# Short unread products on TensorE at five places of a hybrid decoder layer, and second memory rows transposed later

## The chip, the core and the metric

The kernel runs on one core of one Trainium2 chip. The metric is the device time of one execution in microseconds (us). A core has five engines with an instruction stream each: PE (TensorE: matrix products and transposes; its weight loads are listed as PEld), DVE (VectorE), ACT (ScalarE), POOL (GpSimd) and SP (SyncE, which here issues most transfers). An engine works its stream off in order; semaphores hold an instruction until what it needs from another engine, or from a transfer, has landed.

## What is computed

One decoder layer on 1024 rows of 1024 numbers, in float32. Cut to what matters here:

```
# 1. two head groups that share one input projection (2496 columns) and one output projection
cq, ckv, kpe, rq, rk, rv, rg = split(rms_norm(x) @ w_in)
o_mla = causal_block_attention(q(cq), k(ckv, kpe), v(ckv))      # 4 heads
o_ret = retention_chunkwise(rope(rq), rope(rk), rv) -> norm, gain, * silu(rg)   # 4 heads
x1 = x + concat(o_mla, o_ret) @ w_out
# 2. attention to 256 memory rows
kv = rms_norm(mem) @ w_kv;  q = rms_norm(x1) @ w_q
x2 = x1 + softmax(q k^T) v @ w_o
# 3. router: best of 4 groups, best 2 of its 8 experts; 32 experts of width 256
h = rms_norm(x2)
g_sel = argmax(h @ w_group + b);  top2 of h @ w_expert within the group
out = x2 + sum_e gate_e * ((silu(h @ w_gate[e]) * (h @ w_up[e])) @ w_down[e])
```

## The kernel before

Rows go through in eight blocks of 128. Nearly every product is made of three passes (`mm3`, line 144): a matrix is split into a high part H and a low part L (ACT makes H, DVE makes L), and H*H, H*L and L*H are added up in PSUM. `project` (line 200) does that over eight blocks of 128 inputs for up to 512 columns. Rows are turned by PE with an identity matrix (`transposes`, line 160) into a PSUM bank, from which ACT and DVE write the two parts.

The stages in the order of time, with the times at which the profile shows them:

- Start (`phase_a`, 0 to some 40 us): blocks of x are transposed and multiplied by the 448 columns of the latents. The identity arrives by a transfer.
- Retention (`phase_b`, to about 290 us): four heads of retention. Into the last head the keys of the causal attention are interleaved: `kv_products(tb)` multiplies the latent of block tb (names ckvH, ckvL) by `wk` and leaves raw keys `kn`; `kv_keys` scales and transposes them later. At the end comes `out_part(0, ...)`, line 786: the retention half of the output projection for the first row block, 24 products of 512 columns with weights wh and wl and data oT, under the priority name `bout`.
- Causal attention (`phase_c`, to about 530 us): queries from cq, scores, softmax, values, and the other `out_part`s.
- Memory (`phase_e0` and `phase_e1`, to about 584 us): two blocks of memory rows, normed and transposed into `mT[0]` and `mT[1]`, and their projection in four column chunks; with the first chunk both blocks are multiplied one after the other.
- Cross attention (`phase_e`, from 586.93 us): the first two row blocks of x1 are transposed in two halves (i = 0 and 1), then `queries(0, i)` multiplies them by the query weights, 48 products of 256 columns.
- Router and output (`phase_f`, `choose`, `count`, `route_end`, to about 868 us): for the last pair of row blocks two products with the router's weights `wr`, then DVE picks the experts (`ind`, `oh`), PE counts places with small bf16 products (`trib`, `ones`, into the bank ps_trb), DVE builds A and B, PE multiplies them to the lists of rows (ps_po), and POOL gathers the rows `xg` of the first expert with indirect transfers. Only then can PE transpose xg (`expert_x`, line 1440).
- Experts (`moe`, 868 us to the end): 32 experts, each with transposes of the gathered rows, gate and up products, and the down product.

The order on each engine is not that of the code. A scheduler places the instructions when the kernel is built: it goes by priorities, which the table `PRI` shifts by name (`at`, line 219), by its own estimates of when an operand is there, and by extra order edges (`after`, line 207). A new edge or a new instruction can therefore move many others.

Of the kernel before, what the change touches and what calls it, by code (L numbers as in the profile page):

```python
# [26 lines left out]
BF = mybir.dt.bfloat16  # L27
# [10 lines left out]
NT = 8  # L38
EPS = 1e-6
NE = 32  # L40
# [19 lines left out]
AHEAD = 2  # L60
PRI = {'asq': -60, 'bgate': -20, 'bgate1': -15, 'bnorm': 75, 'bout': 200, 'bproj': 15, 'bproj3': -20, 'btr3': 30, 'ckv': -30, 'cpv': -100, 'cpv3': 5, 'cpv6': 10, 'cq3': 400, 'cq6': -10, 'csm': -5, 'csm6': 10, 'cval': -5, 'e1': -100, 'e1t': -60, 'ebl': 30, 'ecv': -60, 'ecw': 13, 'efn': 15, 'eout': -5, 'eout0': 5, 'eq1': 15, 'eqt': 400, 'esm': -100, 'etr': -5, 'fbeg': -12, 'fbeg1': 100, 'fc0': -20, 'fc02': 10, 'fco': 15, 'fco1': -2, 'fl0': -15, 'fl1': 20, 'fl11': 400, 'fl13': -400, 'ft12': -30, 'ftr': -10, 'ftr1': 2, 'ftr3': 2, 'fwe': -400, 'fwe1': 15, 'fwe2': 20, 'fwe3': 5, 'ma': -200, 'mt': -40, 'outa': -60, 'outa4': 20, 'outa5': 5, 'outr': -105, 'outr5': -5, 'q0': 20, 'wal': 15, 'wap': 100, 'wq': -55}
EO = 2
# [43 lines left out]
class Layer:  # L106
# [37 lines left out]
    def mm3(self, out, sH, sL, mH, mL, start, stop, skip=False):  # L144
        mm = lambda s, m, i, e: self.nc.tensor.matmul(out, s, m, start=i, stop=e, skip_group_check=skip)  # L145
        mm(sH, mH, start, False)
        mm(sH, mL, False, False)
        mm(sL, mH, False, stop)

# [10 lines left out]
    def transposes(self, dst, src, n):  # L160
        for i in range(n):
            self.nc.tensor.transpose(dst[:, i * 128:(i + 1) * 128], src[:, i * 128:(i + 1) * 128], self.ident)

# [67 lines left out]
    def constants(self):  # L231
        nc, a, sm = self.nc, self.a, self.sm
        self.ident = sm.tile([128, 128], F32, name="ident", bufs=1)
        nc.scalar.dma_start(self.ident, a["c_ident"])
        self.mhalf = sm.tile([128, 1], F32, name="mhalf", bufs=1)
        nc.gpsimd.memset(self.mhalf, -0.5)
        warm = sm.tile([128, 1], F32, name="warm", bufs=1)
        nc.gpsimd.tensor_tensor(warm, self.mhalf, self.mhalf, OP.mult)
        nc.gpsimd.tensor_tensor(warm, warm, self.mhalf, OP.pow)
        self.gain = {}  # L240
        self.load_gain("attn_norm_g", 8, nc.scalar)
# [118 lines left out]
    def phase_a(self):  # L360
# [13 lines left out]
        for tb in range(NT):  # L374
# [14 lines left out]
            for i in range(2):  # L389
                cols = slice(i * 512, (i + 1) * 512)  # L390
                tr = self.bank(("tr", "sc")[i])
                self.transposes(tr, xt[i], 4)
                self.split(H[:, cols], L[:, cols], tr)
            self.xT.append([(H[:, k * 128:(k + 1) * 128], L[:, k * 128:(k + 1) * 128]) for k in range(8)])
# [9 lines left out]
        for tb in range(NT):  # L404
            p = self.bank("pj", 448)
            self.project(p, self.xT[tb], wc)
            c = self.slot([128, 512], name=("mr", "xr")[tb % 2], bufs=1, pool=self.O)[:, :448]
            nc.scalar.activation(c, p, AF.Copy, scale=self.r1[:, tb:tb + 1])
            for i, (o, n) in enumerate(((0, 256), (256, 128), (384, 64))):
                self.square(self.css[:, tb, i:i + 1], c[:, o:o + n], p[:, o:o + n])  # L410
            nc.sync.dma_start(self.cd[tb * 128:(tb + 1) * 128, :], c)
            if "c" in self.dbg:
                nc.sync.dma_start(self.dbg["c"][tb * 128:(tb + 1) * 128, :], c)
# [166 lines left out]
    def kv_products(self, tb, role):  # L580
# [9 lines left out]
        p = self.bank(role)  # L590
        self.mm3(p, *cT, *self.wk, True, True)
        p = p.rearrange("p (h c) -> p h c", h=NH)
# [193 lines left out]
    def out_part(self, tb, w, ret, role):  # L786
# [14 lines left out]
        for c in range(2):  # L801
            cols = slice(c * 512, (c + 1) * 512)
            xr = self.slot([128, 512], F32, "xr", 1, self.O) if ret is not None else self.slot([128, 512], F32, "xa", XA)
            nc.sync.dma_start(xr, self.a["x"][0][rows, cols] if ret is not None else self.x1d[rows, cols])
            p = self.bank(role)
            self.project(p, oT, w[c])
            nc.vector.tensor_tensor(xr, p, xr, OP.add)
            nc.sync.dma_start(self.x1d[rows, cols], xr)
            if ret is None:
                self.square(self.sx1[:, tb, c:c + 1], xr, p)  # L810
                if "x1" in self.dbg:
                    nc.sync.dma_start(self.dbg["x1"][rows, cols], xr)
# [9 lines left out]
    def phase_e0(self):  # L822
# [10 lines left out]
        for m in range(2):  # L833
# [7 lines left out]
            self.scaled("mt", mt, mt, sq[:, 3:4])  # L841
            self.mT.append(self.to_T(mt, 8, "mT", 4, pool=self.E0))
        self.ggc = ggc

    def phase_e1(self):
# [45 lines left out]
    def phase_e(self):  # L891
# [20 lines left out]
        def queries(n, i):  # L912
# [142 lines left out]
    def phase_f(self):  # L1055
# [74 lines left out]
        def end(j):  # L1130
# [12 lines left out]
            if last:  # L1143
                column(NT - 1, 1, slice(4, 8), slice(256, 512))
                h = rest()
                for k in range(2):
                    nc.tensor.matmul(pl[:, 1], h[:, k], self.wr[:, 6 + k], start=False, stop=(k == 1),
                                     skip_group_check=True)
                nc.vector.scalar_tensor_tensor(v[:, 1:2], self.s2l, 1.0 / D, v[:, 1:2], OP.mult, OP.add)
# [117 lines left out]
    def choose(self, j):  # L1267
# [26 lines left out]
        V.tensor_tensor(ind, oh[:, :, 0], oh[:, :, 1], OP.add)  # L1294
        pr = self.bank("pr", 2 * NE).rearrange("p (b e) -> p b e", b=2)
        for b in range(2):
            nc.tensor.matmul(pr[:, b], self.ones, self.cum[:, j], start=True, stop=False)
            if b:
                nc.tensor.matmul(pr[:, b], self.ones, ind[:, 0], start=False, stop=False)
            nc.tensor.matmul(pr[:, b], self.trib, ind[:, b], start=False, stop=True)  # L1300
        wr = t([2, NE], "wr2")
# [50 lines left out]
    def list_part(self, pl, j, s, first, last, late=lambda i: i):  # L1352
# [14 lines left out]
        for k in range(4):  # L1367
            nc.tensor.matmul(pl[:CAP, s * NE:(2 * s + 1) * NE], A[:, k // 2, k % 2], B[:, k // 2, k % 2],
                             start=first and k == 0 and s == 0, stop=last and k == 3, skip_group_check=True)

# [15 lines left out]
    def route_end(self):  # L1386
# [3 lines left out]
        pc = self.bank("pr", NE)  # L1390
        nc.tensor.matmul(pc, self.ones, self.cum[:, NT // 2], start=True, stop=True)
        self.cnt = G.tile([128, 1], F32, name="cnt", bufs=1)
# [47 lines left out]
    def expert_x(self, xg):  # L1440
# [3 lines left out]
        for b in range(2):  # L1444
            tr = self.bank("tr")
            for k in range(4):
                nc.tensor.transpose(tr[:, k * CAP:(k + 1) * CAP], xg[:CAP, 4 * b + k::8], self.ident[:CAP, :CAP])
            H, L = [self.M.tile([128, 4 * CAP], F32R, name="x" + s, tag="x" + s, bufs=3) for s in "HL"]
# [253 lines left out]
```

## Time and profile before

| | us |
|---|---|
| median of 3 runs | 1211.96 (1209.45 to 1214.25) |
| the profiled execution, its own time | 1214.96 |
| span in that profile, first to last instruction | 1213.2 |
| TensorE busy in the span | 1162.8 |
| VectorE busy | 771.3 |
| ScalarE busy | 652.3 |
| GpSimd busy | 152.0 |

The profile is of one execution. The span leaves out some 1.8 us around it. The mean granted clock of TensorE over the span is 0.986 of full speed. "Busy" adds up instruction times; PE products overlap one another, so what a product costs is read from the distance of two starts, not from the length of one.

### The profile page before, as it was taken

How to read it: one execution, taken by the hardware profiler on the slowest of the kernel's cores; microseconds unless marked ns; L12 is line 12 of the kernel's file. 1: busy time of each engine (PE TensorE's matmuls, PEld its weight loads, DVE VectorE, ACT ScalarE, POOL GpSimd, SP SyncE). 2: the span in 40 equal slices, each digit the busy share in tenths (PEclk: the TensorE clock that was granted, in tenths of full speed). 3: DMA queues.
4: the chain of work that ended last, by engine and by line, in shares of the span. 5: the costliest groups of instructions: out<-in, count | busy, mean ns of one | idle time of the engine just before them, and what ended most of it. 6: DMA issues, size and time to landing. Idle time of an engine off the chain costs nothing. (4 is left out here: it accounts for less than half of the span.)

```text
span 1213.2 us, 18340 instructions
## 1 busy us (share of the span) xinstructions
PE 1162.8 (96%) x6325; PEld 910.7 (75%) x6325; DVE 771.3 (64%) x1938; ACT 652.3 (54%) x1508; POOL 152.0 (13%) x152
## 2 busy tenths in 40 slices
PE   8999999998999999989999999999699999999995
PEld 7887878776688888878899998778565655566552
DVE  5646464678675786658644445555677777777672
ACT  8723232446554664557644446322477777777672
POOL 1011010121100000000000000000222222222222
PEclk9999999999999999999999999999799999999998
DMA  7622020204323433276611024985799999999982
GB/s 237 181 58 80 11 76 10 89 21 132 100 87 104 153 96 120 81 243 191 218 62 62 27 62 150 314 287 210 263 343 343 342 337 334 315 317 315 320 294 45
DMA packets 115472, 213.23 MB, mean 176 GB/s; under 512 B 20577, under 2 KB 68705, under 8 KB 107185
## 3 DMA queue, kind: packets, MB, share of 16 engines
q1 hardware_dynamic: 106912, 194.59, 47.0%
q0 software_dynamic: 7280, 17.37, 6.2%
q8 instruction: 51, 0.84, 0.3%
q14 instruction: 45, 0.36, 0.1%
q10 hardware_dynamic: 1184, 0.07, 0.1%
HBM read 179.69 MB, written 40.11 MB: 181 GB/s over the span
## 5 line engine op out<-in xcount | busy, mean ns | idle before, releaser
L145 PE MATMUL ps_pj<-wh,xT 128*128 128x512 f32 (+1 forms) x640 | 219.9, 403 | 1.8 <-ACT wh L157 1.2
L158 DVE SCALAR_TENSOR_TENSOR L<-raw,g,H 128x512 fp32r<-128x512 f32 x256 | 180.4, 748 | 55.1 <-ACT H L157 52.2
L157 ACT ACTIVATE H<-raw,g 128x512 fp32r<-128x512 f32 x256 | 169.5, 713 | 32.1 <-PE ps_pj L145 22.7
L145 PEld LDWEIGHTS ps_pj<-wh,xT 128*128 128x128 f32 x640 | 121.1, 190 | 21.1 <-ACT wh L157 1.6
L145 PE MATMUL ps_pj<-wl,xT 128*128 128x512 f32 (+1 forms) x320 | 127.9, 400 | 0.0
L1500 PE MATMUL ps_sc<-raw,aT 128*96 128x512 f32 x256 | 117.6, 602 | 1.2 <-ACT aT L1484 1.0
L145 PE MATMUL ps_pj<-H,xH 128*96 128x512 f32 x256 | 116.2, 454 | 0.0
L145 PE MATMUL ps_pj<-L,xH 128*96 128x512 f32 x256 | 102.6, 401 | 0.1
L145 PE MATMUL ps_pj<-H,xL 128*96 128x512 f32 x256 | 102.0, 398 | 0.0
L1500 PEld LDWEIGHTS ps_sc<-raw,aT 128*96 128x96 f32 x256 | 39.1, 162 | 65.1 <-issue 51.1
L1492 POOL DMA_INDIRECT out_dram<-y,idx x31 | 54.4, 1756 | 201.4 <-ACT H L157 161.6
L145 PE MATMUL ps_pj<-x1TH,wh 128*128 128x256 f32 x256 | 74.3, 290 | 2.6 <-ACT x1TH L154 2.6
L145 PE MATMUL ps_pj<-x1TL,wh 128*128 128x256 f32 x256 | 75.2, 294 | 0.0
L145 PE MATMUL ps_pj<-x1TH,wl 128*128 128x256 f32 x256 | 74.4, 291 | 0.0
L145 PEld LDWEIGHTS ps_pj<-wl,xT 128*128 128x128 f32 x320 | 61.1, 191 | 8.5 <-DVE wl L158 0.5
L145 PEld LDWEIGHTS ps_pj<-H,xH 128*96 128x96 f32 x256 | 42.5, 166 | 22.3 <-issue 7.5
L459 ACT ACTIVATE tg<-ps_pj,rh 128x128 f32<-128x128 f32 x32 | 11.7, 366 | 87.7 <-PE ps_pj L145 87.6
L145 PEld LDWEIGHTS ps_pj<-L,xH 128*96 128x96 f32 x256 | 41.7, 163 | 22.4 <-DVE L L158 8.6
L145 PEld LDWEIGHTS ps_pj<-H,xL 128*96 128x96 f32 x256 | 41.5, 162 | 16.0 <-issue 0.7
L145 PEld LDWEIGHTS ps_pj<-x1TH,wh 128*128 128x128 f32 x256 | 48.4, 189 | 3.0 <-ACT x1TH L154 3.0
L1030 ACT ACTIVATE cP<-ps_sc,cnb,fcq 128x256 f32<-128x256 f32 x32 | 17.8, 561 | 57.9 <-DVE cnb L1025 57.9
L145 PEld LDWEIGHTS ps_pj<-x1TH,wl 128*128 128x128 f32 x256 | 48.6, 190 | 0.0
(412 smaller groups left out, 2882.3 us busy)
## 6 DMA issues: line engine op xcount, KB each, us to landing
raw<-in_expert_w_down_dram SPq DMA_DIRECT2D x32, 1024.0 KB
raw<-in_expert_w_gate_dram SPq DMA_DIRECT2D x32, 1024.0 KB
raw<-in_expert_w_up_dram SPq DMA_DIRECT2D x32, 1024.0 KB
raw<-in_w_in_dram SPq DMA_DIRECT2D x32, 256.0 KB
raw<-in_cross_w_kv_dram SPq DMA_DIRECT2D x32, 256.0 KB
x<-x1d SPq DMA_DIRECT2D x16, 512.0 KB
xr<-in_x_dram SPq DMA_DIRECT2D x16, 256.0 KB
raw<-in_w_out_dram SPq DMA_DIRECT2D x16, 256.0 KB
```

Of the source, the lines that this page charges most:

```text
L145: mm = lambda s, m, i, e: self.nc.tensor.matmul(out, s, m, start=i, stop=e, skip_group_check=skip)
L157: self.high = nc.scalar.activation(H, src, AF.Copy, scale=scale)
L158: return nc.vector.scalar_tensor_tensor(L, src, scale, H.bitcast(F32), OP.mult, OP.subtract)
L459: nc.scalar.activation(tg, p[:, 384:512], AF.Tanh, scale=rh[:, tb:tb + 1])
L1030: nc.scalar.activation(P[:, js], s[:, js], AF.Exp, bias=nb[:, j:j + 1], scale=f[:, j:j + 1], accum_out=su[:, j:j + 1])
L1492: add = lambda c, cs: sums.append(nc.gpsimd.indirect_dma_start(out=out, out_offset=bass.IndirectOffsetOnAxis(ap=rows[:, c:c + 1], axis=0), ...
L1500: nc.tensor.matmul(py[:CAP], act[:, j * CAP:(j + 1) * CAP], wd[:, j, cs], start=(j == 0), stop=(j == 1))
```

## The change

A new helper `idle(out, n, earlier, x)` issues n products of 128x128 whose result nobody reads, into a PSUM bank that is about to be overwritten or lies spare. Its data is the float32 identity, or at the start a bf16 tile `fill` that POOL sets to ones. The first of them is put behind the instruction `earlier` by an order edge. It is called at these places:

1. Start: 24 bf16 products ahead of the first transposes of x, and 8 ahead of the first projection.
2. `out_part` of the first row block of retention: 7 float32 products, ordered behind `self.ckvT`, which is the last product of whichever `kv_products` was emitted last.
3. Memory: 7 behind the transposes of the first memory block, into the bank of the first projection. The transposes of the second memory block move from `phase_e0` into `phase_e1`, behind the emission of the first projection, with the new priority name `mt1`.
4. Cross attention: 8 ahead of the first query products, behind the last transposes.
5. Router: 10 behind the last `wr` products, 3 behind the last place product, 16 behind the product with `cum`; order edges put the work that follows behind them.

```diff
-PRI = {'asq': -60, ...
+PRI = {'mt1': 14, 'asq': -60, ...
...
-            self.nc.tensor.transpose(dst[:, i * 128:(i + 1) * 128], src[:, i * 128:(i + 1) * 128], self.ident)
+            self.lastT = self.nc.tensor.transpose(dst[:, i * 128:(i + 1) * 128], src[:, i * 128:(i + 1) * 128],
+                                                  self.ident)
+
+    def idle(self, out, n, earlier, x=None):
+
+        x = self.ident if x is None else x
+        for _ in range(n):
+            i = self.nc.tensor.matmul(out[:, :128], x, x, start=True, stop=True, skip_group_check=True)
+            if earlier:
+                self.after(i, earlier, "where TensorE waits")
+            earlier = i
+        return i
...
+        self.fill = sm.tile([128, 128], BF, name="fill", bufs=1)
+        nc.gpsimd.memset(self.fill, 1.0)
...
+                if tb == i == 0:
+                    self.idle(tr, 24, None, self.fill)
                 self.transposes(tr, xt[i], 4)
+                if tb == 0:
+                    first = self.lastT
...
+            if tb == 0:
+                self.idle(p, 8, first, self.fill)
             self.project(p, self.xT[tb], wc)
...
-        self.mm3(p, *cT, *self.wk, True, True)
+        self.ckvT = self.mm3(p, *cT, *self.wk, True, True)
...
+            if c == tb == 0 and ret is not None:
+                self.idle(p, 7, self.ckvT)
             self.project(p, oT, w[c])
...
-            self.mT.append(self.to_T(mt, 8, "mT", 4, pool=self.E0))
-        self.ggc = ggc
+            if m == 0:
+                self.mT.append(self.to_T(mt, 8, "mT", 4, pool=self.E0))
+                self.p0 = self.bank("pj")
+                self.idle(self.p0, 7, self.lastT)
+        self.ggc, self.mem1 = ggc, mt
...
-                p = self.bank("pj")
+                p = self.bank("pj") if c or m else self.p0
                 self.project(p, mT[m], wc)
+                if c == m == 0:
+                    with self.at("mt1"):
+                        mT.append(self.to_T(self.mem1, 8, "mT", 4, pool=self.E0))
...
+                if n == 0:
+                    self.idle(p[n], 8, self.lastT)
...
+                self.spare = self.bank("pj")
+                self.idled = self.idle(self.spare, 10, i)
...
+            if last and b:
+                self.after(i, self.idled, "where TensorE waits")
...
+        if last:
+            self.idled = self.idle(self.spare, 3, i)
...
+            if last and s == 0 and self.idled:
+                self.after(i, self.idled, "where TensorE waits")
...
+        i = nc.tensor.matmul(pc, self.ones, self.cum[:, NT // 2], start=True, stop=True)
+        self.idled = self.idle(self.spare, 16, i)
...
+                if self.idled:
+                    self.after(i, self.idled, "where TensorE waits")
+                    self.idled = None
```

Three places show how the order moves on PE. The first is the end of retention. Before, the products with oT of `out_part(0)` begin right behind the key product (ckv) of row block 6, and the chain of the last two blocks (transposes of kn and wk, and what follows) is interleaved with them:

```order
L145 MATMUL ps_pjp<-wh,ckvH 128x512
L145 MATMUL ps_pjp<-wl,ckvH 128x512
L145 MATMUL ps_pjp<-wh,ckvL 128x512
L145 MATMUL ps_pj<-wh,oTH 128x512
L145 MATMUL ps_pj<-wl,oTH 128x512
L145 MATMUL ps_pj<-wh,oTL 128x512
L145 MATMUL ps_pj<-wh,oTH 128x512
L145 MATMUL ps_pj<-wl,oTH 128x512
L145 MATMUL ps_pj<-wh,oTL 128x512
L162 MATMUL ps_trp<-ident,kn 128x128 x4
```

After, PE goes from block 6's key product straight to the chain (transposes of kn, of wk, of the latents, the query products of cq, transposes of qn). Here is the end of that chain, with the key product of block 7 and what stands behind it:

```order
L162 MATMUL ps_trp<-ident,qn 128x128 x2
L145 MATMUL ps_pjp<-wh,ckvH 128x512
L145 MATMUL ps_pjp<-wl,ckvH 128x512
L162 MATMUL ps_trp<-ident,qn 128x128 x2
L145 MATMUL ps_pjp<-wh,ckvL 128x512
L169 MATMUL ps_pj<-ident 128x128 x7
L145 MATMUL ps_pj<-wh,oTH 128x512
L145 MATMUL ps_pj<-wl,oTH 128x512
```

The seven unread products and the 24 products with oT stand behind block 7's key product; the scores of the causal attention that were ahead of it stand behind them.

The second is the entry of cross attention on PE, where x1TH and x1TL are the transposed rows of x1 and x the rows themselves. Before:

```order
L145 MATMUL ps_pj<-wh,mTL 128x512
L145 MATMUL ps_pj<-x1TH,wh 128x256
L162 MATMUL ps_tr<-ident,x_6628 128x128 x4
L162 MATMUL ps_tr<-ident,x_6630 128x128 x4
L145 MATMUL ps_pj<-x1TL,wh 128x256
```

After, in the same place:

```order
L145 MATMUL ps_pj<-wh,mTL 128x512
L162 MATMUL ps_tr<-ident,x_6676 128x128 x4
L162 MATMUL ps_tr<-ident,x_6678 128x128 x4
L169 MATMUL ps_pj<-ident 128x128 x8
L145 MATMUL ps_pj<-x1TH,wh 128x256
L145 MATMUL ps_pj<-x1TL,wh 128x256
```

The first query product no longer stands ahead of the second half's transposes, and the eight unread products lie between these and it.

The third is the router's end on PE (wr: router weights; trib, ones: counting; B and A: lists; xg: gathered rows), after the change; without the rows of line 169 these rows stand as before:

```order
L1176 MATMUL ps_sc<-wr,h 128x36 x2
L169 MATMUL ps_pj<-ident 128x128 x10
L1334 LDWEIGHTS trib
...
L1334 MATMUL ps_trb<-ind,trib 128x32
L169 MATMUL ps_pj<-ident 128x128 x3
L1406 MATMUL ps_po<-B,A 96x32 x4
L1431 LDWEIGHTS ones
L1431 MATMUL ps_trb<-cum,ones 128x32
L169 MATMUL ps_pj<-ident 128x128 x16
L1488 MATMUL ps_tr<-ident,xg_10031 128x96 x8
```

Each group stands ahead of the instruction that waited before.

## Rows read from the trace of the kernel before

**Rows 1.** Page, busy us of each engine, share of the span, instructions:

```profile
PE 1162.8 (96%) x6325; PEld 910.7 (75%) x6325; DVE 771.3 (64%) x1938; ACT 652.3 (54%) x1508; POOL 152.0 (13%) x152
```

**Rows 2.** TensorE's waits: total us, times, longest; six of the longest:

```profile
PE ps_tr L1447 <- DMA xg<-x2d,src: 4.1, 1, 4.1
PE ps_tr L162 <- DMA ident<-in_c_ident_dram: 3.9, 1, 3.9
PE ps_trb L1300 <- DVE ind L1294: 3.1, 1, 3.1
PE ps_pj L145 <- DVE oTL L155: 2.7, 1, 2.7
PE ps_pj L145 <- ACT x1TH L154: 2.6, 1, 2.6
PE ps_pj L145 <- ACT mTH L154: 2.4, 1, 2.4
...
PE ps_po L1368 <- DVE A L1359: 1.3, 1, 1.3
```

**Rows 3.** Windows: start:end, length, busy us by engine, then PEclk, DMA:

```profile
283.30:304.90 21.60, 17.65 (x91) 14.24 (x92) 17.32 (x54) 10.41 (x35) 3.48 (x4) 0.92 0.53 173
304.90:320.00 15.10, 12.43 (x67) 8.38 (x65) 10.64 (x36) 9.00 (x31) 1.08 (x2) 1.00 0.26 94
...
340.00:520.00 180.00, 176.99 (x1134) 154.57 (x1133) 123.12 (x324) 96.30 (x246) 5.04 (x5) 1.00 0.34 109
...
584.30:590.00 5.70, 3.11 (x15) 2.95 (x15) 4.01 (x7) 4.08 (x8) 0.00 (x0) 0.70 0.50 162
...
861.00:868.30 7.30, 1.29 (x9) 0.97 (x8) 6.16 (x31) 2.68 (x5) 3.50 (x3) 0.50 0.62 209
868.30:873.60 5.30, 5.26 (x24) 4.05 (x24) 3.81 (x10) 2.13 (x4) 2.96 (x4) 0.54 0.90 243
```

**Rows 4.** Timeline of the start, TensorE: start us, length, operation:

```profile
11.50 0.57 PE L145 MATMUL ps_pj<-wh,xT 128*128 128x448 f32 x1
11.87 1.05 PE L162 MATMUL ps_sc<-ident,xin 128*128 128x128 f32 x4
```

**Rows 5.** The same stretch on ScalarE, idle time in brackets:

```profile
11.36 0.60 ACT L154 ACTIVATE xT<-ps_tr 128x512 fp32r<-128x512 f32 x1 [0.91 <-PE ps_tr L162]
...
12.96 0.60 ACT L154 ACTIVATE xT<-ps_sc 128x512 fp32r<-128x512 f32 x1 [1.00 <-PE ps_sc L162]
```

**Rows 6.** Timeline of TensorE, end of retention:

```profile
290.22 0.40 PE L145 MATMUL ps_pj<-wh,oTH 128*128 128x512 f32 x1
290.45 0.40 PE L145 MATMUL ps_pj<-wl,oTH 128*128 128x512 f32 x1
...
294.12 0.38 PE L481 MATMUL ps_sc<-w 128*128 128x128 f32 x2
294.34 0.39 PE L489 MATMUL ps_st<-w,wk 128*128 128x128 f32 x2
...
295.59 0.38 PE L162 MATMUL ps_tr<-ident,wk 128*128 128x128 f32 x2
...
304.54 0.48 PE L145 MATMUL ps_pjp<-wh,ckvL 128*128 128x512 f32 x1
```

**Rows 7.** Timeline of TensorE, first memory products:

```profile
536.16 0.78 PE L145 MATMUL ps_pj<-wh,mTH 128*128 128x512 f32 x1
...
538.80 0.39 PE L145 MATMUL ps_pj<-wh,mTH 128*128 128x512 f32 x1
```

**Rows 8.** Timeline of TensorE, entry of cross attention:

```profile
587.34 1.97 PE L162 MATMUL ps_tr<-ident,x 128*128 128x128 f32 x8
...
590.06 0.28 PE L145 MATMUL ps_pj<-x1TH,wh 128*128 128x256 f32 x1
```

**Rows 9.** Timeline of TensorE, counting products of the router:

```profile
861.02 0.19 PE L1297 MATMUL ps_trb<-cum,ones 128*128 128x32 bf16 x1
861.05 0.19 PE L1299 MATMUL ps_trb<-ind,ones 128*128 128x32 bf16 x1
```

More of the change, by code (lines that the diff above doesn't have):

```diff
@@ L60 @@
 AHEAD = 2
-PRI = {'asq': -60, 'bgate': -20, 'bgate1': -15, 'bnorm': 75, 'bout': 200, 'bproj': 15, 'bproj3': -20, 'btr3': 30, 'ckv': -30, 'cpv': -100, 'cpv3': 5, 'cpv6': 10, 'cq3': 400, 'cq6': -10, 'csm': -5, 'csm6': 10, 'cval': -5, 'e1': -100, 'e1t': -60, 'ebl': 30, 'ecv': -60, 'ecw': 13, 'efn': 15, 'eout': -5, 'eout0': 5, 'eq1': 15, 'eqt': 400, 'esm': -100, 'etr': -5, 'fbeg': -12, 'fbeg1': 100, 'fc0': -20, 'fc02': 10, 'fco': 15, 'fco1': -2, 'fl0': -15, 'fl1': 20, 'fl11': 400, 'fl13': -400, 'ft12': -30, 'ftr': -10, 'ftr1': 2, 'ftr3': 2, 'fwe': -400, 'fwe1': 15, 'fwe2': 20, 'fwe3': 5, 'ma': -200, 'mt': -40, 'outa': -60, 'outa4': 20, 'outa5': 5, 'outr': -105, 'outr5': -5, 'q0': 20, 'wal': 15, 'wap': 100, 'wq': -55}
+PRI = {'mt1': 14, 'asq': -60, 'bgate': -20, 'bgate1': -15, 'bnorm': 75, 'bout': 200, 'bproj': 15, 'bproj3': -20, 'btr3': 30, 'ckv': -30, 'cpv': -100, 'cpv3': 5, 'cpv6': 10, 'cq3': 400, 'cq6': -10, 'csm': -5, 'csm6': 10, 'cval': -5, 'e1': -100, 'e1t': -60, 'ebl': 30, 'ecv': -60, 'ecw': 13, 'efn': 15, 'eout': -5, 'eout0': 5, 'eq1': 15, 'eqt': 400, 'esm': -100, 'etr': -5, 'fbeg': -12, 'fbeg1': 100, 'fc0': -20, 'fc02': 10, 'fco': 15, 'fco1': -2, 'fl0': -15, 'fl1': 20, 'fl11': 400, 'fl13': -400, 'ft12': -30, 'ftr': -10, 'ftr1': 2, 'ftr3': 2, 'fwe': -400, 'fwe1': 15, 'fwe2': 20, 'fwe3': 5, 'ma': -200, 'mt': -40, 'outa': -60, 'outa4': 20, 'outa5': 5, 'outr': -105, 'outr5': -5, 'q0': 20, 'wal': 15, 'wap': 100, 'wq': -55}
 EO = 2
@@ L147, in mm3 @@
         mm(sH, mL, False, False)
-        mm(sL, mH, False, stop)
+        return mm(sL, mH, False, stop)
     def split(self, H, L, src, scale=None):
@@ L1146, in end @@
                 for k in range(2):
-                    nc.tensor.matmul(pl[:, 1], h[:, k], self.wr[:, 6 + k], start=False, stop=(k == 1),
-                                     skip_group_check=True)
+                    i = nc.tensor.matmul(pl[:, 1], h[:, k], self.wr[:, 6 + k], start=False, stop=(k == 1),
+                                         skip_group_check=True)
+                self.spare = self.bank("pj")
+                self.idled = self.idle(self.spare, 10, i)
                 nc.vector.scalar_tensor_tensor(v[:, 1:2], self.s2l, 1.0 / D, v[:, 1:2], OP.mult, OP.add)
@@ L1295, in choose @@
         pr = self.bank("pr", 2 * NE).rearrange("p (b e) -> p b e", b=2)
+        last = j == NT // 2 - 1
         for b in range(2):
-            nc.tensor.matmul(pr[:, b], self.ones, self.cum[:, j], start=True, stop=False)
+            i = nc.tensor.matmul(pr[:, b], self.ones, self.cum[:, j], start=True, stop=False)
+            if last and b:
+                self.after(i, self.idled, "where TensorE waits")
             if b:
                 nc.tensor.matmul(pr[:, b], self.ones, ind[:, 0], start=False, stop=False)
-            nc.tensor.matmul(pr[:, b], self.trib, ind[:, b], start=False, stop=True)
+            i = nc.tensor.matmul(pr[:, b], self.trib, ind[:, b], start=False, stop=True)
+            if last and not b:
+                self.after(i, self.idled, "where TensorE waits")
+        if last:
+            self.idled = self.idle(self.spare, 3, i)
         wr = t([2, NE], "wr2")
@@ L1367, in list_part @@
         for k in range(4):
-            nc.tensor.matmul(pl[:CAP, s * NE:(2 * s + 1) * NE], A[:, k // 2, k % 2], B[:, k // 2, k % 2],
-                             start=first and k == 0 and s == 0, stop=last and k == 3, skip_group_check=True)
+            i = nc.tensor.matmul(pl[:CAP, s * NE:(2 * s + 1) * NE], A[:, k // 2, k % 2], B[:, k // 2, k % 2],
+                                 start=first and k == 0 and s == 0, stop=last and k == 3, skip_group_check=True)
+            if last and s == 0 and self.idled:
+                self.after(i, self.idled, "where TensorE waits")
     def list_rows(self, pl):
@@ L1390, in route_end @@
         pc = self.bank("pr", NE)
-        nc.tensor.matmul(pc, self.ones, self.cum[:, NT // 2], start=True, stop=True)
+        i = nc.tensor.matmul(pc, self.ones, self.cum[:, NT // 2], start=True, stop=True)
+        self.idled = self.idle(self.spare, 16, i)
         self.cnt = G.tile([128, 1], F32, name="cnt", bufs=1)
@@ L1446, in expert_x @@
             for k in range(4):
-                nc.tensor.transpose(tr[:, k * CAP:(k + 1) * CAP], xg[:CAP, 4 * b + k::8], self.ident[:CAP, :CAP])
+                i = nc.tensor.transpose(tr[:, k * CAP:(k + 1) * CAP], xg[:CAP, 4 * b + k::8], self.ident[:CAP, :CAP])
+                if self.idled:
+                    self.after(i, self.idled, "where TensorE waits")
+                    self.idled = None
             H, L = [self.M.tile([128, 4 * CAP], F32R, name="x" + s, tag="x" + s, bufs=3) for s in "HL"]
```

## The prediction

> **What bounds the kernel now.** I read the page first: TensorE is busy for 1162.8 of 1213.2 us [rows 1], so only some 50 us of its time are idle, and work added to its stream counts unless it lies in such an idle time. The list of its waits says where these are [rows 2]. Six of them are the five places of the change: 4.1 us for the gathered rows xg, 3.9 for the identity, 3.1 for ind, 2.7 for oTL, 2.6 for x1TH, 2.4 for mTH; 1.3 for A lies between the two of the router. Then windows around these places show the granted clock [rows 3]. It is 0.50 in 861 to 868.3 and 0.54 in 868.3 to 873.6, where TensorE is busy for 5.26 of 5.3 us; 0.70 in 584.3 to 590; 0.92 over 283.3 to 304.9; 1.00 in the long causal stage, whose 180 us hold 177 of work. So behind a wait TensorE works at half its pace for a few us, and a wait costs more than its length. That is what a fill could win; a fill can't end the waits, which end on transfers, DVE or ACT. Last I read timelines there for prices, and the order of the instructions, since the scheduler has placed them anew.
>
> **Prices.** At full pace a product of 512 columns takes 0.23 us from start to start (290.22 to 290.45) [rows 6], at half pace 0.44 (six in 2.64 us from 536.16 to 538.80) [rows 7]. A float32 128x128 product, two passes, takes 0.22 at full pace (294.12 to 294.34) [rows 6], so I put 0.44 at half pace. No row has a bf16 product of 128 columns. Those of 32 columns start 0.03 apart at a granted clock of 0.50 [rows 9, 3]; four times the columns gives 0.12 as an estimate. The upper bound is a float32 transpose of 128 columns at about half pace, 0.25 (eight in 1.97) [rows 8].
>
> **1, the start.** The 24 products need only a small POOL fill, and by 0.12 each they take 2.9 us, inside the 3.9 us wait for the identity; by 0.25 they take 6.0 and end some 2.5 us late, which is the bound of loss. Another 8 lie behind the transposes, where PE would wait for ACT to split them. What can be won: at 11.50 a product of 448 columns takes 0.37, half pace against 512 columns in 0.23 [rows 4, 6]. ACT there waits twice for PE's transposes, 0.91 and 1.00 us [rows 5]; with PE at full pace these go. Later ACT is what is late, so no more than the two is won. I take **-1.9** (range -2.6 to +2.5).
>
> **2, the end of retention.** Here the order decides. The fills are tied to the last `kv_products` emitted, which is block 7's, not block 6's after which the 2.7 us wait stood. So the wait is not filled: the seven fills and the 24 products with oT behind them now stand at the end of the chain of the last two blocks. Before, these 24 were what TensorE did while that chain went through DVE, ACT and POOL: 24 x 0.231 = 5.5 us from 286 on. The chain can't speed up by as much: its transposes of wk ran at 295.59, and these wait for DVE's rotations, whose order there is the same as before. Block 7's key product ends the chain; its last pass started at 304.54 [rows 6]. Without the twelve score passes and the others that the new order puts behind it, 1.6 us earlier: about 302.9. Then 7 x 0.22 = 1.55 and 5.5: 310 us. By 304.9 the kernel before had also done some 2.5 us of scores and other products that now stand behind. The lag is 310 - 304.9 + 2.5 = 7.6 us at full pace; with idle time left in the chain the clock may fall, and at half pace the fills and the first products bring it to 12. What can be caught up afterwards: 304.9 to 320 has 15.10 - 12.43 = 2.67 us of idle time, and 340 to 520 has 3.0 [rows 3]; I take 1 off. 6.6 and 11, weighted two to one: **+8** (range +5 to +12).
>
> **3, the memory.** Seven fills (1.5 us at full pace, 3.1 at half) go into the 2.4 us wait for mTH [rows 2], which ends on ACT's split of the transposes. The products after it lost 2.64 - 6 x 0.23 = 1.25 us by the pace [rows 7]. The second block's eight transposes are issued anyway; between products they cost no more than before. The gain may be lost at the wait for x1TH, if a transfer sets that: 0 to -1.7, I take **-1.2**.
>
> **4, entry of cross attention.** In the new order all eight transposes of the second half come first, then the eight fills, then the products. The fills are not in the 2.6 us wait [rows 2] but behind it. At half pace 8 x 0.44 = 3.5 us; the pace in the trace returned at 590.06, the seventh product [rows 8], so a part runs at full: transposes to 588.9, fills to about 591.2. By then the kernel before had done 16 products, some at half pace, that now take 16 x 0.12 = 1.9. I take **+2**. At full pace (1.8 us of fills, less about 1.1 of faster transposes) it is +0.7.
>
> **5, the router.** At full pace 10 fills take 2.2, 3 take 0.66, 16 take 3.5 us; the waits are 3.1, 1.3 and 4.1 [rows 2], so they are covered. At half pace the sixteen need 7.0 and the transposes of xg come 2.9 us late; the ten need 4.4 and add 1.3 more. The gain is the half pace after 868.3: 5.26 x (1 - 0.54) = 2.4 us [rows 3]. If the pace doubles within the sixteen, they end about 0.9 late, and -2.4 + 0.9 = **-1.5** (range -2.4 to +4.2).
>
> On the profile's clock the Trainium skill has a rule, TensorE: Matmul & The Clock Gate, section Terms: the penalty of throttling is about the throttled time times what the clock lacks of full. By that rule, an estimate, 584.3 to 590 would give back 5.7 x 0.30 = 1.7 us, 861 to 873.6 some 7.3 x 0.50 + 5.3 x 0.46 = 6.1; the trace does not bear out the second, because TensorE was busy for only 1.29 us of the first 7.3 [rows 3], and the pace lost while waiting costs nothing. By the rule in place of my terms for these two places the sum would be 5.4 - 3.7 - 4.6 = -2.9, or 1209.1 in the median, no change that can be told; it falls together with the rival of a neutral order and shares its chance.
>
> **Sum.** -1.9 + 8 - 1.2 + 2 - 1.5 = +5.4, against the profiled execution of 1214.96: 1220.4. That execution is 3.0 above the median of 1211.96, so I forecast 1220.4 - 3.0 = **1217.4**, about 0.45% slower. A measurement of this kernel can tell about 0.5%, 6.06 us: below 1205.9 is faster, above 1218.0 slower.
>
> **Rivals.**
> - *The fills do what they say and the new order costs nothing.* The end of retention gives -1.6 (the pace lost from 286 to about 290), the entry of cross attention -1.5 by overlap with its wait, the others their best: -2.6 - 1.6 - 1.7 - 1.5 - 2.4 = -9.8, so 1205.2 and **1202.2** in the median. For it: half pace stands behind each wait [rows 3]. Against it: the order at two places. It decides for faster as long as place 2 costs less than about +2.1.
> - *The new order is neutral*: the 24 products fill later idle time as well as they filled the chain. Place 2 is 0, the rest as in the sum: -2.6, **1209.4**. For it: the causal stage has other idle spots, and DVE (17.32 of 21.60 us) is nearly the bound at the end of retention [rows 3].
> - *The fills don't raise the pace.* Short products leave the clock where it was; they run at half pace: 0 + 11 + 0 + 2.2 + 4.2 = +17.4, so **1229.4** in the median. For it: at 868.3 TensorE worked nearly without a gap for 5 us at a mean of 0.54 [rows 3]. It decides at place 5, if the sixteen aren't over when xg lands.
>
> **Chances.** My forecast 0.48, with its own range 1213 to 1222: 0.21 of it slower by over 0.5%, 0.27 within. Half pace 0.10, all slower. Neutral order 0.21: 0.17 within, 0.04 faster. Fills as meant 0.21, faster. Together: faster 0.25, same 0.44, slower 0.31. The range 1203 to 1226 leaves out most of the half-pace case and about half of the best one, 0.18.
>
> **What the profile after would show.** Place 2: TensorE's idle time between block 6's and block 7's key products grows from 4 us (21.60 - 17.65 [rows 3]) to about 10, and the products with oT start near 304 instead of 286. Place 4: the wait for x1T stays at about 2.5, now before a transpose or the fills, and the first product starts near 591. Place 1: ACT's two waits gone, the 448-column products 0.20 apart before 12. Place 5: the clock of the 5 us after xg lands near 1, the wait for xg filled. The prediction is wrong if the products with oT, though late, leave the causal stage's end where it was, or if the sixteen delay xg's transposes by more than the pace gives back.

## The result, and the profile after

The changed kernel takes 1229.59 us (median of 6 runs, 1227.16 to 1233.32) against 1212.51 of the kernel before (6 runs): a ratio of 1.0142, with a 95% interval of 1.0123 to 1.0161. That is 17 us slower, above the end of the range (1226). The profiled execution after has a span of 1227.5 us (1229.36 with what lies around it), 14.3 more than before.

Where the time comes in is read from the first use of a few tiles: the scores of the causal attention (qTH), the memory products (mTH), the query products of cross attention (x1TH), the gathered rows (xg). Here are these rows of the kernel before, by tile (min, median and longest time of one in ns, then the starts of the first and the last in us):

```profile
L145 PE MATMUL ps_sc<-kv,qTH x160: 274/283/388, 302.2 to 503.8; 128*128 128x256 f32 x160
L145 PE MATMUL ps_pj<-wh,mTH x64: 392/394/776, 533.8 to 583.5; 128*128 128x512 f32 x64
L145 PE MATMUL ps_pj<-x1TH,wh x256: 277/282/583, 586.9 to 736.6; 128*128 128x256 f32 x128
L1447 PE MATMUL ps_tr<-ident,xg x256: 246/274/427, 868.3 to 1179.2; 96*128 96x96 f32 x128
```

And of the changed kernel:

```profile
L145 PE MATMUL ps_sc<-kv,qTH x160: 274/282/562, 318.9 to 520.7; 128*128 128x256 f32 x160
L145 PE MATMUL ps_pj<-wh,mTH x64: 392/394/494, 550.6 to 598.8; 128*128 128x512 f32 x64
L145 PE MATMUL ps_pj<-x1TH,wh x256: 278/282/369, 604.5 to 752.8; 128*128 128x256 f32 x128
L1488 PE MATMUL ps_tr<-ident,xg x256: 246/274/349, 883.2 to 1193.9; 96*128 96x96 f32 x128
```

The first scores come 16.7 us later, and the first memory product 16.8 later. Behind that the distance goes up and down and shrinks in the end: 15.3 at the last memory product, 17.6 at the first query product, 16.2 at the last one, 14.9 at the gathered rows. The last pass of block 6's key product, at the end of retention, still comes 0.4 us earlier than before (282.45 against 282.89). So the loss arises between that product and the memory products, which is where place 2 stands, and the other places together look like a gain of some 2 us in these two executions. The stretch between the two points, before and then after (columns as in [rows 3]):

```profile
282.89:533.75 250.86, 237.33 (x1454) 201.27 (x1452) 171.92 (x477) 135.16 (x371) 12.73 (x14) 0.99 0.37 121
282.45:550.62 268.17, 247.18 (x1483) 210.69 (x1481) 172.42 (x477) 136.45 (x371) 12.94 (x14) 0.95 0.35 113
```

It is 17.3 us longer. Of these, 7.5 us are idle time of TensorE and 9.8 are busy time: the unread products that lie in it, and products that ran at the lower clock.

The six long waits [rows 2] are gone from the top of the list of waits; others stand there now (us in total, times, longest):

```profile
PE ps_trp L162 <- DVE kn L627: 5.4, 2, 3.9
PE ps_fl L145 <- DVE xr L828: 3.0, 3, 1.9
PE ps_trp L162 <- DVE kv L155: 3.0, 2, 1.7
PE ps_trp L162 <- ACT qn L667: 2.6, 2, 1.3
PE ps_trp L162 <- DVE kv L158: 2.2, 3, 1.6
PE ps_tr L162 <- DVE x1TL L155: 1.9, 1, 1.9
...
PE ps_tr L1488 <- DMA xg<-x2d,src: 0.4, 1, 0.4
```

The waits for kn, kv and qn are those of the chain at the end of retention and of its continuation. Before, the 24 products stood in this time, and what was left to wait was shorter (0.79 us for qn at 299.54). The wait for xg shrank from 4.1 us to 0.4, because unread products lie in it, and the rows still come no earlier.

TensorE's timeline at place 2, after:

```profile
282.45 0.39 PE L145 MATMUL ps_pjp<-wh,ckvL 128*128 128x512 f32 x1
286.75 0.98 PE L162 MATMUL ps_trp<-ident,kn 128*128 128x128 f32 x4 [3.91 <-DVE kn L627]
...
294.80 0.69 PE L162 MATMUL ps_tr<-ident,wk 128*128 128x128 f32 x2 [0.85 <-DVE wk L493]
...
305.70 0.69 PE L162 MATMUL ps_trp<-ident,qn 128*128 128x128 f32 x2 [1.30 <-ACT qn L667]
...
307.65 0.78 PE L145 MATMUL ps_pjp<-wh,ckvL 128*128 128x512 f32 x1
308.23 2.97 PE L169 MATMUL ps_pj<-ident 128*128 128x128 f32 x14
310.95 0.48 PE L145 MATMUL ps_pj<-wh,oTH 128*128 128x512 f32 x1
...
316.50 0.60 PE L162 MATMUL ps_trp<-ident,kn 128*128 128x128 f32 x4
318.66 0.44 PE L162 MATMUL ps_trp<-ident,krt 128*128 128x128 f32 x2 [1.56 <-DVE kv L158]
318.85 0.48 PE L145 MATMUL ps_sc<-kv,qTH 128*128 128x256 f32 x2
```

The first row is the end of block 6's key product. Behind it TensorE waits 3.9 us for kn, does the chain with gaps and at half pace, and reaches the unread products (14 passes for 7) at 308.23, the products with oT at 310.95 and the end of them at 316.50. Windows of this stretch and of the router's end (columns as in [rows 3]):

```profile
282.80:311.00 28.20, 18.39 (x66) 13.70 (x65) 16.78 (x56) 12.68 (x43) 3.38 (x4) 0.58 0.25 80
311.00:325.00 14.00, 10.71 (x56) 9.07 (x56) 5.41 (x11) 2.68 (x6) 1.01 (x1) 0.88 0.26 94
...
883.20:888.50 5.30, 5.16 (x34) 4.16 (x35) 4.56 (x14) 2.69 (x5) 3.47 (x4) 1.00 0.86 243
```

Against [rows 3], idle time at the end of retention grew from 4.0 to 9.8 us and the granted clock fell from 0.92 to 0.58; behind it another 3.3 us are idle. At the router the clock of the 5.3 us after xg lands is 1.00 in place of 0.54: there the unread products do what they should.

What the other engines do meanwhile shows in ScalarE's first step after the chain, and VectorE's:

```profile
317.13 0.69 ACT L157 ACTIVATE kv<-ps_trp,ggn 128x512 fp32r<-128x512 f32 x1 [6.55 <-PE ps_trp L162]
```

```profile
317.86 0.75 DVE L158 SCALAR_TENSOR_TENSOR kv<-ps_trp,ggn,kv 128x512 fp32r<-128x512 f32 x1 [3.19 <-ACT kv L157]
```

While TensorE works through the unread products and the 24 products, ScalarE stands for 6.55 us for a transpose of kn that is queued behind them, 8.85 us behind the key product's last pass (316.50 against 307.65). Before, the 24 products were done by 294.12, and these transposes came 2.0 us behind that pass (306.50 against 304.54), so ScalarE's wait was short:

```profile
307.17 0.69 ACT L157 ACTIVATE kv<-ps_trp,ggn 128x512 fp32r<-128x512 f32 x1 [0.56 <-PE ps_trp L162]
```

### The profile page after: what moved, and what is told of

Read it like the earlier page. It is cut to its first block, busy times and chain, and to the rows that moved or that the text cites. A ratio compares the mean times of both kernels' runs of the same rounds, so it can differ in the third digit from the quotient of the medians.

```text
span 1227.5 us, 18608 instructions
## 1 busy us (share of the span) xinstructions
PE 1178.0 (96%) x6459; PEld 925.2 (75%) x6459; DVE 771.4 (63%) x1938; ACT 653.8 (53%) x1508; POOL 154.6 (13%) x153
## 5 line engine op out<-in xcount | busy, mean ns | idle before, releaser
L145 PEld LDWEIGHTS ps_pj<-x1TL,wh 128*128 128x128 f32 x256 | 48.3, 189 | 0.0
```

## The experiments

**The place at the end of retention alone, or left out.** Three kernels. `no2` is the changed kernel without it:

```diff
-            if c == tb == 0 and ret is not None:
-                self.idle(p, 7, self.ckvT)
```

> The changed kernel without the seven products at the end of retention (place 2); the other four places stay. Theory, the order at place 2: what was lost came from tying these products, and with them the 24 products with oT, behind block 7's key product. Then this kernel has the trace's differences of the other places alone: about -0.4 at the start, -1.4 at the memory, +0.8 at the entry of cross attention, -0.9 at the router, so -2 of the kernel before, 1210 to 1211, ratio 0.997 to 0.999. Rival, the loss is spread (unread products anywhere cost, or moving the memory transposes does): it stays above 1218, ratio over 1.005.

`only2` is the kernel before with these lines, `ckvT` and `idle`, and nothing else of the change.

> The kernel before with place 2 alone: seven unread products tied behind block 7's key product. Theory, the order at place 2: the whole loss and the small gains of the other places given back, 1229 to 1232, ratio 1.014 to 1.016. Rival, the loss is spread over the places: under 1222, ratio under 1.008.

`one` is `only2` with one unread product in place of seven:

```diff
-                self.idle(p, 7, self.ckvT)
+                self.idle(p, 1, self.ckvT)
```

> As the kernel with place 2 alone, but with one unread product in place of seven; on TensorE the order is else the same. Theory, the order: the place is what costs, six products fewer give back 2.3 us at the 0.39 that they took, so 1226 to 1229. Rival, the unread products themselves cost (their time, or their PSUM bank): most of the loss goes, under 1218.

Measured: `no2` 1.0008 (0.9995 to 1.0020), `only2` 1.0130 (1.0104 to 1.0156), `one` 1.0116 (1.0096 to 1.0135). The whole loss is this place, and it is the tie and not the products: with one product it is nearly the same. In the traces the products take 1.99 us in `only2` (308.07 to 310.06) and 0.28 in `one` (308.06 to 308.34), so six more are 1.7 us; the ratios are 0.0014 apart, which is as much, but their intervals overlap. The range expected of `only2`, 1.014 to 1.016, was missed by a little, and the one of `no2`, 0.997 to 0.999, too: the other four places gave no gain together, so the 2 us that the two traces above seemed to show lie within what two executions differ by.

**The tie moved along the chain.** Where the products with oT are tied was changed. `block6` ties the seven behind block 6's key product, just ahead of the wait:

```diff
-        self.ckvT = self.mm3(p, *cT, *self.wk, True, True)
+        i = self.mm3(p, *cT, *self.wk, True, True)
+        if tb == 6:
+            self.ckvT = i
```

> As the kernel with place 2 alone, but the seven products are tied behind block 6's key product, which stands just ahead of the 2.7 us wait for oTL; the 24 products with oT stay where they were in the kernel before. Theory, the order: the loss is gone, and the half pace from 286 to 290 with it if the products raise the clock: 1209 to 1213, ratio 0.997 to 1.001. Rival, any extra edge or product here makes the scheduler lay out the causal attention anew, and that is what costs: over 1220, ratio over 1.006.

`mid0` and `mid` have one unread product tied inside the chain, behind the transposes of cq (`cqT`) and behind its first six products (in the same line, `cq0`):

```diff
-                self.idle(p, 7, self.ckvT)
+                self.idle(p, 1, self.cqT)
```

> Place 2 alone with one unread product, tied not behind block 7's key product but earlier in the same chain, behind the transposes of the latents cq (at 295 us in the kernel before). The 24 products with oT follow it. Theory, the cover: these products were the work that TensorE did while the chain of the last two blocks went through the other engines; tied here they leave the first 10 us of the chain bare and still cover its second half, so the loss is about half of that with the tie behind block 7: 6 to 9 us, ratio 1.005 to 1.008. Rival, any tie that takes the products out of their place makes the scheduler lay out what follows worse, however far it takes them: 1.010 to 1.013 as with the tie behind block 7.

> As mid0, but tied behind the first six query products of cq (some 299 us with the chain at half pace). Theory, the cover: more of the chain is bare than in mid0 and less than with the tie behind block 7: 8 to 12 us, ratio 1.007 to 1.010, and above mid0. Rival: 1.010 to 1.013, equal to mid0.

Measured, with the start of the first product with oT from each trace:

| tied behind | products with oT from | ratio (95%) |
|---|---|---|
| nothing (before) | 286.02 us | 1 |
| block 6's key product, 7 products | 289.92 | 1.0033 (1.0017 to 1.0050) |
| transposes of cq, 1 product | 297.17 | 1.0076 (1.0052 to 1.0101) |
| six products of cq, 1 product | 299.42 | 1.0083 (1.0061 to 1.0105) |
| block 7's key product, 1 product | 308.34 | 1.0116 (1.0096 to 1.0135) |
| block 7's key product, 7 products | 310.06 | 1.0130 (1.0104 to 1.0156) |

The loss grows with the distance, from 4 us for 3.9 to 14 for 22.3. Neighbours in the table can't be told apart, since their intervals overlap; but all eight times of `mid0` and `mid` (1219.0 to 1225.6) lie below all eight of `one` and `only2` (1225.8 to 1233.2), against medians of the kernel before that are 0.3 us apart. That is what the cover theory says; the rival, that any tie which takes the products out of their place costs the same, falls. A weaker rival stays. In each of these kernels TensorE also does the causal attention in another order than before, with the same products. The cost doesn't follow how far that reaches: the old order is back from 379 us on in `mid0`, and only from 473 on in `block6`, which lost less. But what the new order costs by itself was not isolated.

The tie that was expected to cost nothing, `block6`, also cost 4 us (2.1 to 6.1), between the ranges of its theory and its rival. A part of the reason is in its trace:

```profile
283.16 0.39 PE L145 MATMUL ps_pjp<-wh,ckvL 128*128 128x512 f32 x1
286.29 2.73 PE L169 MATMUL ps_pj<-ident 128*128 128x128 f32 x12 [2.74 <-DVE oTL L155]
288.82 1.06 PE L162 MATMUL ps_trp<-ident,kn 128*128 128x128 f32 x4
289.67 0.49 PE L169 MATMUL ps_pj<-ident 128*128 128x128 f32 x2
289.92 0.47 PE L145 MATMUL ps_pj<-wh,oTH 128*128 128x512 f32 x1
```

The unread products don't lie in the wait: they start when it ends, at 286.29, with the same 2.74 us before them that the real products had [rows 2]. They write a bank of ps_pj, of which the kernel has three in this stage (`self.psum(pj=3, ...)`). VectorE's steps that read ps_pj there:

```profile
285.46 0.68 DVE L155 TENSOR_TENSOR oTL<-ps_pj,oTH 128x512 fp32r<-128x512 f32 x1
287.73 0.28 DVE L484 TENSOR_TENSOR wk<-ps_pj,sn 128x128 f32<-128x128 f32 x1
288.00 0.28 DVE L474 SCALAR_TENSOR_TENSOR sg<-tg,ps_pj 128x128 f32<-128x128 f32 x1
```

TensorE wrote nothing else to ps_pj between 282.9 and 286.29, so the last two still read older products, and two banks were held beyond 286.29. The one that came free is that of the first row: the unread products waited for the step that makes oTL, as the real ones did. So they fill nothing and push the first product with oT back by 3.6 us. That push is not the whole account of the 4 us: block 7's key product comes only 1.5 us later than before (305.47 against 303.93), and further on another stretch of this trace is at half pace,

```profile
317.00:324.00 7.00, 6.50 (x22) 5.11 (x23) 3.99 (x10) 2.98 (x9) 0.00 (x0) 0.51 0.39 121
```

where the clock before was 1.00. (Such a stretch can be chance: the same window is at 0.76 in the trace of `only4`, below, whose order on TensorE is that of before up to there.) How the loss divides between the two is open. Whether another bank would have let the products into the wait was not tried.

**The half pace in the bare chain.** `warm20` is `one` with the second column half of the products tied as well, and 20 more unread products that the scheduler may lay between the chain's instructions:

```diff
-            if c == tb == 0 and ret is not None:
-                self.idle(p, 1, self.ckvT)
+            if tb == 0 and ret is not None:
+                if c == 0:
+                    self.idle(p, 20, self.ckv6)
+                self.idle(p, 1, self.ckvT)
```

> As the kernel with one unread product behind block 7's key product, the second column half of the 24 products tied there too, and 20 more unread products laid by the scheduler into the first half of the bare chain (from 286 to about 292 us), where TensorE went at half pace. Theory, the pace: the half pace in the chain is a good part of the loss beside the missing cover; with the first half at full pace block 7's key product starts 1.5 to 3 us before 306, and the ratio falls to 1.007 to 1.010. Rival, the chain waits for the other engines and the pace matters little: block 7's key product stays at 306 to 308, ratio 1.011 to 1.014 as with one product.

Measured 1.0079 (1.0054 to 1.0103). The windows of the same stretch, of `warm20`:

```profile
282.80:308.00 25.20, 17.46 (x99) 14.06 (x98) 16.99 (x55) 11.96 (x40) 3.38 (x4) 0.90 0.28 94
```

and of `one`:

```profile
282.80:308.00 25.20, 14.91 (x51) 10.46 (x51) 15.93 (x54) 10.19 (x34) 3.38 (x4) 0.61 0.29 90
```

The clock rose from 0.61 to 0.90, and block 7's key product came only 1.3 us earlier (first pass, of `warm20` and then of `one`):

```profile
304.91 0.47 PE L145 MATMUL ps_pjp<-wh,ckvH 128*128 128x512 f32 x1 [0.24 <-DVE rt L540]
```

```profile
306.22 0.76 PE L145 MATMUL ps_pjp<-wh,ckvH 128*128 128x512 f32 x1
```

The ratio is in the theory's range, but the key product is a little later than the theory had it. Part of what the pace gave was taken on the way there, since the transposes of cq, in the middle of the chain, came later in `warm20`. They are shown for `one` and then for `warm20`:

```profile
295.44 0.63 PE L162 MATMUL ps_trp<-ident,cq 128*128 128x128 f32 x2
```

```profile
296.16 0.44 PE L162 MATMUL ps_trp<-ident,cq 128*128 128x128 f32 x2 [0.16 <-DVE ckvL L155]
```

From there to the key product the chain took 10.8 us in `one` and 8.8 in `warm20`, against 8.1 in the kernel before (295.81 to 303.93), so in that half the pace is some 2 us. The ratio fell by 0.0037, or 4.5 us, but the two intervals overlap. The stretch from block 6's key product to the first memory product, of `one` and then of `warm20`:

```profile
282.63:548.12 265.49, 242.90 (x1457) 206.61 (x1455) 172.43 (x477) 136.16 (x371) 12.93 (x14) 0.95 0.36 114
```

```profile
282.90:546.49 263.59, 243.16 (x1499) 208.34 (x1497) 172.59 (x477) 136.13 (x371) 12.92 (x14) 0.99 0.36 115
```

Against the kernel before, `one` is 14.6 us longer there, 9.1 of idle and 5.6 of busy time; `warm20` is 12.7 longer, 6.9 and 5.8: its clock is nearly that of before, but its 21 further unread products are busy time too. So idle time is the larger part of the loss. How much of the 14 us is pace was not settled: the traces show 1.3 to 2 us of it, and the ratios leave room for 4.5.

**The other places, one at a time.** Each is the kernel before with one place of the change, cut from its diff: `only1` the start, `only3` the memory, `only4` the entry of cross attention, `only5` the router. The first added line of each, in this order:

```diff
+                    self.idle(tr, 24, None, self.fill)
...
+                self.idle(self.p0, 7, self.lastT)
...
+                    self.idle(p[n], 8, self.lastT)
...
+                self.idled = self.idle(self.spare, 10, i)
```

> The kernel before with place 1 alone: 24 and 8 unread bf16 products at the start. The four places other than the end of retention gave 1.0008 together, so each is small or they cancel. My term for this one was -1.9 us (ratio 0.998); the trace of the changed kernel shows the end of retention only 0.4 us earlier, which would be 0.9996. Theory, what is won ahead of a stage that ScalarE or a transfer bounds is given back: 0.999 to 1.001. Rival, my term: 0.997 to 0.999.

> The kernel before with place 3 alone: seven unread products in the wait for the first memory block, and the second block's transposes moved behind the first projection. My term was -1.2 us (ratio 0.999). Theory, the products after it do run at full pace, but the first of them starts later, because more of its stream now stands ahead: 0.999 to 1.001. Rival, my term in full or more: 0.997 to 0.999.

> The kernel before with place 4 alone: eight unread products behind the second half's transposes, ahead of the first query products. My term was +2 us (ratio 1.0017), since they stand behind the wait. Theory, the eight transposes already bring the pace back, and the eight products only add themselves: 1.000 to 1.002. Rival, they give back the half pace of the first query products in full: 0.998 to 0.999.

> The kernel before with place 5 alone: 10, 3 and 16 unread products in the router's waits. My term was -1.5 us (ratio 0.9988), from half pace after the gathered rows land. Theory, the profile shows that gain at the first expert's products, but the experts that follow are bound by more than TensorE's start: 0.999 to 1.001. Rival, my term in full: 0.997 to 0.999.

Measured: `only1` 0.9998 (0.9986 to 1.0009), `only3` 0.9999 (0.9990 to 1.0007), `only4` 1.0018 (1.0005 to 1.0030), `only5` 0.9992 (0.9980 to 1.0004). Two show no difference, one a loss of 2.2 us, and 1.0 us at the router may be nothing. In the trace of `only1` the gain at the start is there, and is given back on the way:

```profile
L145 PE MATMUL ps_sc<-kv,qTH x160: 277/283/387, 299.8 to 503.2; 128*128 128x256 f32 x160
L145 PE MATMUL ps_pj<-wh,mTH x64: 392/394/794, 534.1 to 584.4; 128*128 128x512 f32 x64
```

The first scores come 2.4 us earlier than before, the last 0.6 earlier, and the first memory product 0.3 later, behind a wait for mTH that is now 3.3 us long. By this trace, what is won ahead of the causal attention is taken by waits in it and behind it; but that is likely and not shown, since the last scores come at 506.2 in the execution of `only5` and at 503.8 in that of the kernel before, with the same order up to there. `only4`, where before the seventh product started at 590.06 [rows 8]:

```profile
588.59 1.78 PE L162 MATMUL ps_tr<-ident,x 128*128 128x128 f32 x8 [4.00 <-DVE x1TL L155]
590.16 3.16 PE L169 MATMUL ps_pj<-ident 128*128 128x128 f32 x16
593.08 0.36 PE L145 MATMUL ps_pj<-x1TH,wh 128*128 128x256 f32 x1
```

The unread products stand behind the wait and take 2.9 us of their own. The wait ahead of them is 4.0 us long in this trace, against 2.6 before.

**The fourth place moved into its wait.** `four_early` is `only4` tied behind the last memory product:

```diff
-                    self.idle(p[n], 8, self.lastT)
+                    self.idle(p[n], 8, self.kvlast)
```

> Place 4 alone, with its eight unread products tied behind the last product of the memory projection in place of the last transposes, so that seven of them stand inside the wait for x1TH and not behind it. Theory, the position: the +2 us of place 4 are the products behind the wait; here the wait covers them: 0.999 to 1.001. Rival, the new order of transposes and first products at this place costs by itself: 1.001 to 1.003 as before.

Measured 1.0003 (0.9988 to 1.0018): no loss is left that can be told, though the interval still reaches the 1.0018 of `only4`, and no gain took its place. Its trace has them where they should be:

```profile
585.66 1.72 PE L169 MATMUL ps_pj<-ident 128*128 128x128 f32 x14
587.22 0.60 PE L162 MATMUL ps_tr<-ident,x 128*128 128x128 f32 x4
```

**Versions without what loses.** `p135` has the start, the memory and the router; `p1345e` also the fourth place as in `four_early`.

> The kernel before with the places that did not lose by themselves: the start, the memory, the router. If their measured ratios multiply: 0.9998 x 0.9999 x 0.9992 = 0.9989, between 0.997 and 1.000. Rival, what one wins another wait takes: 0.9995 to 1.001.

> The start, the memory and the router as changed, and the entry of cross attention with its products tied behind the last memory product, inside the wait; the end of retention as before. If the measured ratios multiply: 0.9988 x 1.0003 = 0.999, between 0.997 and 1.0005, clearer than without place 4 only if the pace at that entry counts. Rival, the place is worth nothing or less there: over 1.0.

Measured 0.9988 (0.9975 to 1.0001) and 0.9988 (0.9974 to 1.0003). Both are at the product of the single ratios; both intervals reach 1, so a gain of 1.5 us is likely and not shown.

## Why the prediction was wrong

The direction was forecast and the place was the right one: the tie to block 7's key product leaves the chain of the last two blocks bare. The step that failed is the size of **term 2**, +8 with a range of +5 to +12; alone it measures 1.0130, or +15.8 us (12.6 to 18.9). By its own steps:

- "About 302.9" for the last pass of block 7's key product, from which the fills were counted. That pass starts at 307.65 and the fills at 308.23, 5.3 us later. I took the times of the kernel before and subtracted the work that the new order puts behind, as if the chain got shorter by it. But TensorE waits in it for other engines: twice 1.30 us for qn and 0.85 for wk. From the transposes of cq to the first pass of the key product the chain took 8.1 us before; in `warm20`, near full pace, it took 8.8, so the 1.6 us that I subtracted did not come off. In the changed kernel it took 11.1 (295.28 to 306.38), and the 2.3 us on top of 8.8 are the half pace, which I had put on the fills and the first products and not on the chain.
- "7 x 0.22 = 1.55 and 5.5". The seven took 2.72, at half pace for the most part; the 24 took 5.55 (310.95 to 316.50), as worked out. So these end at 316.5 and not at 310. Put into the prediction's own formula that is 316.5 - 304.9 + 2.5 = 14.1 us, in place of 7.6 at full pace and 12 at half.
- "I take 1 off" for what is caught up afterwards. Nothing shows that it was: the place alone measures 15.8. ScalarE stood still for 6.55 us while the 24 products ran, and when they were over, TensorE waited again for kv: 3.3 us idle from 311 to 325. I had looked for idle time on TensorE that the late work could use, and not for work of ScalarE and VectorE that is queued behind it. That this makes up the rest of the miss is likely and not shown.
- The two cases, full pace 6.6 and half pace 11, were both too low; the weighting between them was not what failed. The rival with half pace gave 1229.4, near the measured 1229.6, but that is luck: it put +11 on place 2, +4.2 on the router and +2.2 on place 4, and at the router the clock did rise.

The other terms against what each measures alone: the start -1.9, measured -0.2 (-1.7 to +1.1); the memory -1.2, measured -0.1 (-1.2 to +0.8); the entry of cross attention +2, measured +2.2 (0.6 to 3.6); the router -1.5, measured -1.0 (-2.4 to +0.5). The sum of the single measurements is +16.7, and the change measures +17.1, so the places add up. **Term 4** was right in size and reason, as the position behind the wait shows. **Term 3** is neither borne out nor refuted: in the trace of `only3` the memory products take 48.9 us from the first to the last, in place of 49.7, and -1.2 lies at the edge of the interval. **Term 5** was right about the clock (0.54 to 1.00), and its -1.5 lies in the interval; from the first transposes of xg to the first down product it is 16.1 us before, 14.9 in `only5` and 14.6 in the changed kernel. By the Trainium skill's rule for the penalty (TensorE: Matmul & The Clock Gate, section Terms), worked out ahead as an estimate of 6.1 us for that stretch, the gain would have been several times what was measured (1.0, at most 2.4); the prediction's reading of the trace, that pace lost while waiting is worth nothing, agrees with it. **Term 1** failed as a sum over a stage's own waits: in `only1` ScalarE's two waits shrank from 0.91 and 1.00 us to 0.16 and 0.25, and block 6's key product came 1.3 us earlier, but the kernel's time did not show it; by that trace it came back as a longer wait 230 us later.

What the profile was to show: the idle time of place 2, said to be about 10 us, is 9.8; the products with oT, said to start near 304, start at 310.95; the wait for x1T, said to stay at about 2.5, is 1.9; the clock after xg is near 1, as said. The rivals: that the fills work and the order is free fell with `only2`; that the new order is neutral fell with it too; that the fills don't raise the pace fell at the router.

## What to carry to other kernels

Work that an engine does out of turn may be the cover of a chain that runs through the other engines. Before tying an instruction to a later one, ask what fills the time between the two, and whether other engines have steps queued behind the work that is moved: the cost here was the length that was left bare, at half pace for a part of it, and then the waits when everything started again at its end.

Before an unread product is put into a wait, ask whether anything it touches is part of that wait. Here a bank that was still being read (`block6`) and an edge to an instruction behind the wait (place 4) each made it one more product behind the wait.

A raised clock is worth the pace of the work that then follows on the path, and in a kernel of many stages a us won early may only be waited out later.

## What was not expected of the hardware

Keeping the clock up was worth little here even where it worked. At the router the granted clock went from 0.54 to 1.00 for 5.3 us with TensorE busy for 5.2 of them, and with that place alone, whose trace has the clock at 1.00 there too, the time changed by -1.0 us (-2.4 to +0.5). In the bare chain it went from 0.61 to 0.90 over 25 us and its end came 1.3 us earlier, of the 14 us that the tie cost.
